# Seven products of a column-block pair summed in three PSUM banks that are read in between

## The chip, the core and the metric

The kernel runs on one core of a Trainium2 chip. The metric is the device time of one execution in microseconds (us): the median of three runs of the kernel before is 2645.06 us (2643.67 to 2646.84).

## The reference

The reference is a decoder trunk of two layers over one sequence of 1024 tokens with 1024 features, in float32. Each layer has a mixer and a gated MLP, both behind an RMSNorm that is shifted, scaled and gated by columns computed from a conditioning vector (adaLN).

```python
proj = h @ w_in                       # mixer: 4 retention heads, 4 HGRN2 heads, 128 wide
rq, rk, rv, rg, hq, hf, hi, hg = jnp.split(proj, idx, axis=-1)
...
merged @ w_out
...
a = h @ w_gate                        # MLP, 2816 wide
acc = causal_conv3(a) + conv_b
(jax.nn.silu(acc) * (h @ w_val)) @ w_down
```

Nearly all the arithmetic lies in `h @ w_in`, `h @ w_gate` and `h @ w_val`: every 128 columns of such a weight give 128 features for 1024 tokens.

## The kernel before

Activations are held feature-major: 128 features on the partitions, 1024 tokens along a row, in tiles Z of 128 x 1024 (12 of them, handed out and given back in a first-in, first-out list). Every operand of a large matmul is split exactly into two parts (hi and lo), so that a block of 128 x 128 weights against 512 tokens takes three matmuls: hi by hi, hi by lo, lo by hi (L451 to L453).

Most column blocks are computed in pairs. `pair` (L456) takes two blocks of 128 columns, a "gate" block g and a "value" block v, and gets their products with all 1024 tokens by seven products of halves in place of eight (the scheme of Strassen and Winograd). The halves of the activation (`b11`, `b12`, `b21`, `b22`) and their sums (`tops[1]` to `tops[3]`) are prepared once per norm by `sum_operands` and `last_operand`. The halves of the weights and their sums are made for each pair: GpSimd adds (L463 to L469), and `piece` (L324 on) splits each of the seven with one ScalarE copy (L329) and one VectorE subtraction (L330) into a rotation of six buffers. The raw weights of the two blocks come by two DMAs on SP's queue into two buffers, which are free again when the last split that reads them is done.

A product (`product`, L447) is 12 matmuls of 128x128 by 128x512 that are summed in one PSUM bank. I call the products P1 to P7 after the weight piece that they use. The banks come from a rotation of four (`pr_ps`); four more (`at_ps`) serve the mixer's small matmuls. In an ordinary pair the order is P1, P6, P2, P7, P4, P5, P3. P1 is copied to v0 by ScalarE (L491); each later result is added on VectorE to a half of g or v (L485), P5 twice (L485, L510). The first pair of each MLP has `plain_first` set: its order is P1, P2, P3, P6, P7, P4, P5, since the sums of the operands come late there; P3 is copied too (L497), and GpSimd does one add (L501). There are 68 pairs, 34 in each layer: 14 in the mixer, 20 in the MLP.

After each result `step` (L384) lets other work go on: a tick of the adaLN sums (VectorE, L165 and L167, for the columns that come later; they run through the first layer's mixer and MLP only) and the next part of the attention chains. `hgrn_chain` (L661) works on the pair f (as g) and q (as v); it has seven score levels, each with TensorE matmuls (L712, L722), a VectorE selection (L714) or ScalarE copy (L724), and two VectorE products (L730, L731). `ret_chain` (L621) turns the pair q, k by rotary (L613 to L618) and then multiplies them (L638). `value_chain` transposes the values. In the MLP `conv_act` (L950 on) takes g through a convolution (ScalarE L954, VectorE L955 and L957, ScalarE L959), multiplies it by v (L965) and stores the result in DRAM; the down projection (`slot_mm`, L526 to L528) loads it again and splits it (L531, L532).

The order of the instructions on each engine is set by the framework's scheduler when the program is made: it simulates the program and puts on each engine what is ready first, the earlier in the program and the work marked `hp()` (weights, copies and adds of the pairs) ahead of the rest. On the chip every engine then works through its own queue in that fixed order, and a wait holds up what stands behind it. The framework adds the waits: an instruction that writes a tile or a bank waits for those that still read it.

Of the kernel before, what the change touches and what calls it, by code (L numbers as in the profile page):

```python
# [29 lines left out]
HALF = 512  # L30
# [10 lines left out]
def kernel(  # L41
# [33 lines left out]
    def pr_ps(name):  # L75
        return psum.tile([P, HALF], F32, tag="pr", name=name)
# [25 lines left out]

# [1 line left out]
    vec_c0 = [("c", c_in.rearrange("b (r p) -> (b r) p", p=P), 8)]  # L104
# [37 lines left out]

# [1 line left out]
    mod = const.tile([P, DEPTH * 48], F32, name="mod")  # L144
# [69 lines left out]

# [1 line left out]

# [107 lines left out]

# [1 line left out]
    def piece(src, n, nm):  # L326
        hi = stg.tile([P, HALF], F32R, tag="whi", bufs=NW, name=f"whi{nm}")
        lo = stg.tile([P, HALF], F32R, tag="wlo", bufs=NW, name=f"wlo{nm}")
        A.activation(hi[:, 0:n], src, AF.Copy)  # L329
        V.tensor_tensor(out=lo[:, 0:n], in0=src, in1=hi[:, 0:n], op=ALU.subtract)  # L330
        return [(hi[:, i:i + P], lo[:, i:i + P]) for i in range(0, n, P)]
# [45 lines left out]
    def need(n):  # L377
        for _ in range(100):
            if len(zfree) >= n:
                return  # L380
            step()
        raise RuntimeError(f"{len(zfree)} of {n} tiles free")
# [27 lines left out]

# [1 line left out]
    def split(dst, k, src):  # L412
# [33 lines left out]

    def product(w, b, nm):  # L447
        ps = pr_ps(nm)
        for k in range(4):
            (wh, wl), rh, rl = w[k], b[0][:, k, :], b[1][:, k, :]  # L450
            T.matmul(ps, wh, rh, start=k == 0, stop=False)  # L451
            T.matmul(ps, wh, rl, start=False, stop=False)  # L452
            T.matmul(ps, wl, rh, start=False, stop=k == 3)  # L453
        return ps

    def pair(src_g, src_v, nm, plain_first=False):  # L456
        rg = load_raw(src_g, KT, nm + "g")
        rv = load_raw(src_v, KT, nm + "v")
        a11, a12, a21, a22 = rg[:, 0:HALF], rg[:, HALF:S], rv[:, 0:HALF], rv[:, HALF:S]
        s1 = stg.tile([P, HALF], F32, tag="s1", bufs=2, name=f"s1{nm}")  # L460
        with hp():
            p1 = piece(a11, HALF, nm + "1")
            G.tensor_add(s1, a21, a22)  # L463
            G.tensor_sub(a21, a11, a21)
            G.tensor_sub(a11, s1, a11)
            if not plain_first:
                p6 = piece(a11, HALF, nm + "6")
            p2 = piece(a12, HALF, nm + "2")
            G.tensor_sub(a12, a12, a11)  # L469
            if plain_first:  # L470
                p3 = piece(a12, HALF, nm + "3")
                p6 = piece(a11, HALF, nm + "6")
            p7 = piece(a21, HALF, nm + "7")
            p4 = piece(a22, HALF, nm + "4")
            p5 = piece(s1, HALF, nm + "5")
            if not plain_first:
                p3 = piece(a12, HALF, nm + "3")
        need(2)
        g, v = Z(), Z()
        g0, g1, v0, v1 = g.t[:, 0:HALF], g.t[:, HALF:S], v.t[:, 0:HALF], v.t[:, HALF:S]  # L480

        def add(o, x, w, b, i):
            ps = product(w, b, f"{nm}_{i}")
            with hp():
                V.tensor_add(o, x, ps)  # L485
            step()
            return ps

        m1 = product(p1, b11, nm + "_1")
        with hp():  # L490
            A.activation(v0, m1, AF.Copy)  # L491
        step()
        if plain_first:
            add(g0, v0, p2, b21, 2)
            m3 = product(p3, b22, nm + "_3")
            with hp():
                A.activation(g1, m3, AF.Copy)  # L497
            step()
            add(v0, v0, p6, tops[2], 6)
            with hp():  # L500
                G.tensor_add(g1, g1, v0)  # L501
            add(v1, v0, p7, tops[3], 7)
        else:
            add(g1, v0, p6, tops[2], 6)
            add(g0, v0, p2, b21, 2)
            add(v1, g1, p7, tops[3], 7)
        add(v0, v1, p4, b12, 4)
        m5 = add(v1, v1, p5, tops[1], 5)
        with hp():
            V.tensor_add(g1, g1, m5)  # L510
        if not plain_first:
            add(g1, g1, p3, b22, 3)
        return g, v
# [19 lines left out]

# [1 line left out]
    def transpose8(src, nm, evac):  # L535
# [222 lines left out]

# [1 line left out]
    xs = [Z() for _ in range(KT)]  # L760
# [85 lines left out]
    for l in range(DEPTH):  # L846
# [1 line left out]
        early = []  # L848
# [95 lines left out]

# [1 line left out]
        ada_all()  # L946
# [49 lines left out]

# [1 line left out]
        places = (sum([slots(b) for b in (b11, tops[2], b21, tops[3])], []), sum([slots(b) for b in (b12, b22, b11, b21)], []),  # L998
# [142 lines left out]
```

## Time and profile before

| | |
|---|---|
| median of 3 runs | 2645.06 us |
| the profiled execution: span from its first to its last instruction | 2637.6 us |
| TensorE matmul busy | 2519.4 us, 96% |
| VectorE busy | 1839.7 us, 70% |
| ScalarE busy | 986.1 us, 37% |
| GpSimd busy | 592.0 us, 22% |
| mean granted TensorE clock | 0.980 |

The profiled execution's own time is known by its span; what lies around the span (launch and end) is not in it. Engines are named PE (TensorE matmul), PEld (its weight load), DVE (VectorE), ACT (ScalarE), POOL (GpSimd) and SP. L451 is line 451 of the kernel. Matmuls are pipelined: one of 128x128 by 128x512 is shown as 0.39 us long, but they begin 0.23 us apart. In a row, the part behind the arrow in brackets names the instruction that ended the engine's idle time.

### The profile page before, as it was taken

Reading aid. Unit: us, or ns where it says so; the run is one execution under the profiler, and the core shown is the slowest. Engines: PE = TensorE matmul, PEld = TensorE weight load, DVE = VectorE, ACT = ScalarE, POOL = GpSimd, SP = SyncE. Lnnn points to the kernel's source line nnn. Section 1 sums busy time; section 2 is a strip of 40 time slices with the busy share of each in tenths; the row PEclk is TensorE's granted clock in tenths of the full one; section 3 lists DMA queues with packets and bytes.
Section 4 is the critical chain, followed back from the end, with each engine's and each line's share of the span. In section 5 each row is a group of like instructions: output and inputs, shape, how many; then the busy total and the mean of one; then the engine's idle time right before and its main releaser. Section 6 shows DMA issues by size and latency. Waiting matters only on the chain.

```text
span 2637.6 us, 32740 instructions
## 1 busy us (share of the span) xinstructions
PE 2519.4 (96%) x12189; PEld 2072.7 (79%) x12189; DVE 1839.7 (70%) x2781; ACT 986.1 (37%) x1685; POOL 592.0 (22%) x480
## 2 busy tenths in 40 slices
PE   5889999999999999899999899999999999999998
PEld 4777877877788888788877788888877888887887
DVE  6988788765987788834377777777387677674435
ACT  4533433333533333412264334444154333342224
POOL 1512223210423323200023222222033332320000
PEclk8999999999999999999999999999999999999999
DMA  8222322552234344732231112224212222254213
GB/s 293 69 86 86 104 77 82 174 187 80 71 121 132 126 140 151 245 125 94 86 108 56 50 39 64 73 73 160 92 56 76 84 76 88 80 198 138 96 53 107
DMA packets 293920, 283.56 MB, mean 108 GB/s; under 512 B 10793, under 2 KB 240769, under 8 KB 293761
## 3 DMA queue, kind: packets, MB, share of 16 engines
q1 hardware_dynamic: 275904, 219.42, 26.7%
q0 software_dynamic: 17408, 61.88, 6.5%
q8 instruction: 96, 1.57, 0.2%
q14 instruction: 63, 0.52, 0.1%
q10 hardware_dynamic: 449, 0.17, 0.0%
HBM read 229.00 MB, written 52.43 MB: 107 GB/s over the span
## 4 chain that ended last, share of the span: by engine, by line
PE 71%; DVE 12%; issue 10%; POOL 4%; DMA 2%; ACT 2%; POOLq 0%; SPq 0%; DVEq 0%; ACTq 0%
PE f L451 6%; PE f L453 6%; PE f L452 6%; PE dn L528 4%; PE dn L526 4%; PE dn L527 4%; PE lh L712 2%; PE wo L526 2%; PE wo L528 2%; PE wo L527 2%; PE g L451 2%; PE g L452 2%; PE g L453 2%; PE dn_last L526 2%; PE dn_last L528 2%
## 5 line engine op out<-in xcount | busy, mean ns | idle before, releaser
L451 PE MATMUL f<-hhi,whif 128*128 128x512 f32 x640 | 253.8, 397 | 1.9 <-DVE z L485 1.8
L453 PE MATMUL f<-hhi,wlof 128*128 128x512 f32 x640 | 251.4, 393 | 0.0
L452 PE MATMUL f<-hlo,whif 128*128 128x512 f32 x640 | 250.1, 391 | 0.0
L485 DVE TENSOR_TENSOR z<-z,f 128x512 f32<-128x512 f32 x238 | 161.5, 682 | 63.1 <-PE f L453 54.0
L451 PE MATMUL f<-thi,whif 128*128 128x512 f32 x480 | 190.2, 396 | 6.0 <-ACT z L491 4.0
L452 PE MATMUL f<-tlo,whif 128*128 128x512 f32 x480 | 190.0, 396 | 0.0
L453 PE MATMUL f<-thi,wlof 128*128 128x512 f32 x480 | 189.7, 395 | 0.0
L528 PE MATMUL dn<-hhi,wlodn 128*128 128x512 f32 x384 | 151.8, 395 | 9.8 <-DVE wlodn L330 9.8
L526 PE MATMUL dn<-hhi,whidn 128*128 128x512 f32 x384 | 151.6, 395 | 0.0
L527 PE MATMUL dn<-hlo,whidn 128*128 128x512 f32 x384 | 150.1, 391 | 0.0
L167 DVE SCALAR_TENSOR_TENSOR ac<-aw,cact,ac 128x512 f32<-128x512 f32 x140 | 130.7, 934 | 22.8 <-DMA aw<-in_ada_w_dram 22.0
L912 DVE SCALAR_TENSOR_TENSOR z<-dn,mod,z 128x512 f32<-128x512 f32 x64 | 48.0, 750 | 136.3 <-PE dn L528 136.1
L453 PEld LDWEIGHTS f<-hhi,wlof 128*128 128x128 f32 x640 | 120.7, 189 | 28.4
L451 PEld LDWEIGHTS f<-hhi,whif 128*128 128x128 f32 x640 | 120.5, 188 | 28.3 <-DVE z L485 2.3
L452 PEld LDWEIGHTS f<-hlo,whif 128*128 128x128 f32 x640 | 120.6, 188 | 26.9
L451 PEld LDWEIGHTS f<-thi,whif 128*128 128x128 f32 x480 | 90.6, 189 | 29.7 <-ACT z L491 4.9
L915 POOL DMA_DIRECT2D xd<-z x48 | 26.0, 541 | 390.4 <-DVE z L912 362.5
L329 ACT ACTIVATE whidn<-rawdn 128x512 fp32r<-128x512 f32 x64 | 39.5, 627 | 186.1 <-PE dn L527 173.3
L453 PEld LDWEIGHTS f<-thi,wlof 128*128 128x128 f32 x480 | 90.6, 189 | 20.9
L452 PEld LDWEIGHTS f<-tlo,whif 128*128 128x128 f32 x480 | 90.2, 188 | 20.6
L712 PEld LDWEIGHTS lh<-z,z 128*128 128x128 f32 x640 | 80.1, 199 | 24.1 <-issue 19.6
L712 PE MATMUL lh<-z,z 128*128 128x64 f32 x640 | 80.1, 280 | 17.1 <-DVE z L731 16.3
(664 smaller groups left out, 6868.7 us busy)
## 6 DMA issues: line engine op xcount, KB each, us to landing
aw<-in_ada_w_dram SPq DMA_DIRECT2D x160, 256.0 KB, 2.7
acts<-z POOLq DMA_DIRECT2D x44, 512.0 KB, 3.2
z<-acts SPq DMA_DIRECT2D x44, 512.0 KB, 4.3
z<-xd POOLq DMA_DIRECT2D x32, 512.0 KB, 5.7
rawdn<-in_w_down_dram SPq DMA_DIRECT2D x32, 512.0 KB, 3.8
xd<-z POOLq DMA_DIRECT2D x52, 256.0 KB, 2.7
rawdn_last<-in_w_down_dram SPq DMA_DIRECT2D x32, 384.0 KB, 3.4
af<-in_ada_w_dram SPq DMA_DIRECT2D x16, 512.0 KB, 9.9
```

Of the source, the lines that this page charges most:

```text
L167: V.scalar_tensor_tensor(out=a, in0=raw, scalar=cact[:, k:k + 1], in1=a, op0=ALU.mult, op1=ALU.add)
L329: A.activation(hi[:, 0:n], src, AF.Copy)
L451: T.matmul(ps, wh, rh, start=k == 0, stop=False)
L452: T.matmul(ps, wh, rl, start=False, stop=False)
L453: T.matmul(ps, wl, rh, start=False, stop=k == 3)
L485: V.tensor_add(o, x, ps)
L526: T.matmul(ps, a, rh, start=i == 0, stop=False)
L527: T.matmul(ps, a, rl, start=False, stop=False)
L528: T.matmul(ps, b, rh, start=False, stop=i == last)
L712: T.matmul(ps[:, c * 64:(c + 1) * 64].rearrange("p (b t) -> p b t", t=s), k.t[:, cs], qp.t[:, cs].rearrange("p (b t) -> p b t", t=s)[:, 1: ...
L912: V.scalar_tensor_tensor(out=x, in0=ps, scalar=mod[:, l * 48 + gate + d:][:, 0:1], in1=x, op0=ALU.mult, op1=ALU.add)
L915: nc.gpsimd.dma_start(out=dst[d, :, sl], in_=x)
```

## The change

`product` gives way to `add_product`, which writes into a bank that it is given and may add to what the bank holds. A pair takes three banks, x, w and y (with `plain_first` a fourth, u). x takes P1, is copied to g0, then takes P6 on top and is copied to g1, takes P7 on top and is added to v1, takes P4 on top and is copied to v0. w takes P2, which is added to g0. y takes P5 and is copied to v1, takes P3 on top and is added to g1. So an ordinary pair has four ScalarE copies and three VectorE adds. The order of the products becomes P1, P2, P6, P5, P7, P3, P4; with `plain_first` it is P1, P2, P3, P6, P5, P7, P4, with P3 in u and four adds. The weight splits stand in the new order. `step` is still called after each result. Comments that the diff removes elsewhere are left out here.

```diff
@@ -444,14 +444,12 @@
             split(b12, k, xs[4 + k].t[:, 0:HALF])
             xs[4 + k].free()
 
-    def product(w, b, nm):
-        ps = pr_ps(nm)
+    def add_product(ps, w, b, first=True, last=True):
         for k in range(4):
             (wh, wl), rh, rl = w[k], b[0][:, k, :], b[1][:, k, :]
-            T.matmul(ps, wh, rh, start=k == 0, stop=False)
-            T.matmul(ps, wh, rl, start=False, stop=False)
-            T.matmul(ps, wl, rh, start=False, stop=k == 3)
-        return ps
+            T.matmul(ps, wh, rh, start=first and k == 0, stop=False, skip_group_check=True)
+            T.matmul(ps, wh, rl, start=False, stop=False, skip_group_check=True)
+            T.matmul(ps, wl, rh, start=False, stop=k == 3, skip_group_check=True)
 
     def pair(src_g, src_v, nm, plain_first=False):
         rg = load_raw(src_g, KT, nm + "g")
@@ -463,53 +461,53 @@
             G.tensor_add(s1, a21, a22)
             G.tensor_sub(a21, a11, a21)
             G.tensor_sub(a11, s1, a11)
-            if not plain_first:
-                p6 = piece(a11, HALF, nm + "6")
             p2 = piece(a12, HALF, nm + "2")
             G.tensor_sub(a12, a12, a11)
             if plain_first:
                 p3 = piece(a12, HALF, nm + "3")
-                p6 = piece(a11, HALF, nm + "6")
+            p6 = piece(a11, HALF, nm + "6")
+            p5 = piece(s1, HALF, nm + "5")
             p7 = piece(a21, HALF, nm + "7")
-            p4 = piece(a22, HALF, nm + "4")
-            p5 = piece(s1, HALF, nm + "5")
             if not plain_first:
                 p3 = piece(a12, HALF, nm + "3")
+            p4 = piece(a22, HALF, nm + "4")
         need(2)
         g, v = Z(), Z()
         g0, g1, v0, v1 = g.t[:, 0:HALF], g.t[:, HALF:S], v.t[:, 0:HALF], v.t[:, HALF:S]
 
-        def add(o, x, w, b, i):
-            ps = product(w, b, f"{nm}_{i}")
+        def out(o, ps):
             with hp():
-                V.tensor_add(o, x, ps)
+                A.activation(o, ps, AF.Copy)
             step()
-            return ps
-
-        m1 = product(p1, b11, nm + "_1")
-        with hp():
-            A.activation(v0, m1, AF.Copy)
-        step()
+
+        def add(o, ps):
+            with hp():
+                V.tensor_add(o, o, ps)
+            step()
+
+        x, w, y = pr_ps(nm + "_x"), pr_ps(nm + "_w"), pr_ps(nm + "_y")
+        add_product(x, p1, b11)
+        out(g0, x)
+        add_product(w, p2, b21)
+        add(g0, w)
         if plain_first:
-            add(g0, v0, p2, b21, 2)
-            m3 = product(p3, b22, nm + "_3")
-            with hp():
-                A.activation(g1, m3, AF.Copy)
-            step()
-            add(v0, v0, p6, tops[2], 6)
-            with hp():
-                G.tensor_add(g1, g1, v0)
-            add(v1, v0, p7, tops[3], 7)
-        else:
-            add(g1, v0, p6, tops[2], 6)
-            add(g0, v0, p2, b21, 2)
-            add(v1, g1, p7, tops[3], 7)
-        add(v0, v1, p4, b12, 4)
-        m5 = add(v1, v1, p5, tops[1], 5)
-        with hp():
-            V.tensor_add(g1, g1, m5)
+            u = pr_ps(nm + "_u")
+            add_product(u, p3, b22)
+        add_product(x, p6, tops[2], False)
+        out(g1, x)
+        if plain_first:
+            add(g1, u)
+        add_product(y, p5, tops[1])
+        out(v1, y)
+        if plain_first:
+            add(g1, y)
+        add_product(x, p7, tops[3], False)
+        add(v1, x)
         if not plain_first:
-            add(g1, g1, p3, b22, 3)
+            add_product(y, p3, b22, False)
+            add(g1, y)
+        add_product(x, p4, b12, False)
+        out(v0, x)
         return g, v
 
     def slots(b):
```

## Rows read from the trace of the kernel before

**Rows 1.** The page: span, and busy times (us, share, instructions).

```profile
span 2637.6 us, 32740 instructions
PE 2519.4 (96%) x12189; PEld 2072.7 (79%) x12189; DVE 1839.7 (70%) x2781; ACT 986.1 (37%) x1685; POOL 592.0 (22%) x480
```

**Rows 2.** Windows, mixers then MLPs: us, PE, PEld, DVE, ACT, POOL, clock, DMA.

```profile
112.00:480.00 368.00, 339.48 (x2061) 288.19 (x2062) 304.52 (x523) 133.23 (x286) 92.77 (x59) 0.97 0.31 95
1410.00:1770.00 360.00, 337.73 (x2042) 286.83 (x2041) 266.71 (x461) 134.96 (x289) 90.22 (x59) 0.98 0.18 56
760.00:1060.00 300.00, 299.79 (x1336) 245.18 (x1335) 247.43 (x330) 100.11 (x150) 94.32 (x75) 1.00 0.44 140
2010.00:2350.00 340.00, 340.00 (x1473) 276.82 (x1472) 236.35 (x300) 120.24 (x175) 107.16 (x90) 1.00 0.28 91
```

**Rows 3.** TensorE's waits, whole span: waited for, us in total, times, longest.

```profile
PE lh L712 <- DVE z L731: 16.3, 8, 5.9
...
PE dn L528 <- DVE wlodn L330: 9.8, 2, 7.6
PE v L451 <- ACT z L491: 8.1, 2, 4.1
```

**Rows 4.** Busy times within one MLP pair: second layer, first layer (columns as above).

```profile
2176.50:2196.00 19.50, 19.50 (x86) 15.89 (x85) 13.48 (x17) 6.99 (x11) 6.15 (x5) 1.00 0.25 81
938.30:957.70 19.40, 19.40 (x90) 15.98 (x89) 16.22 (x21) 7.23 (x12) 6.16 (x5) 1.00 0.35 109
```

**Rows 5.** Groups, VectorE: adds of MLP pairs (busy us, mean ns).

```profile
L485 DVE TENSOR_TENSOR z<-z,f 128x512 f32<-128x512 f32 x238 | 161.5, 682 | 63.1 <-PE f L453 54.0 <-issue 7.5
```

**Rows 6.** Timeline: product after P1 begins, copy of P1; MLP 2, MLP 1.

```profile
2179.23 0.40 PE L451 MATMUL f<-thi,whif 128*128 128x512 f32 x1
...
2179.80 0.58 ACT L491 ACTIVATE z<-f 128x512 f32<-128x512 f32 x1
...
941.03 0.40 PE L451 MATMUL f<-thi,whif 128*128 128x512 f32 x1
...
944.84 0.57 ACT L491 ACTIVATE z<-f 128x512 f32<-128x512 f32 x1
```

**Rows 7.** Chain of waits, 1085 to 1112: start us, us, what.

```profile
1092.40 1.23 DVE z L965
...
1100.03 6.43 DMA z<-acts
```

**Rows 8.** Busy times and clock around two of TensorE's waits (columns as above).

```profile
1098.90:1113.30 14.40, 6.75 (x24) 5.09 (x23) 9.72 (x12) 3.24 (x3) 2.10 (x4) 0.76 0.79 295
...
207.00:219.00 12.00, 7.88 (x34) 6.58 (x33) 10.21 (x13) 2.32 (x4) 4.46 (x4) 0.72 0.11 44
```

**Rows 9.** Timeline of VectorE, value pair of head 1, second layer.

```profile
1503.21 1.29 DVE L676 COPY_PREDICATED z<-mkh,z 128x1024 f32<-128x1024 uint8 x1
```

**Rows 10.** Timeline of TensorE, first pair of the first layer.

```profile
109.97 1.11 PE L540 MATMUL tpr_0v<-ident,z 128*128 128x128 f32 x4 [5.32 <-ACT z L606]
```

**Rows 11.** Timeline of TensorE and ScalarE, first MLP pair of the first layer.

```profile
707.62 0.58 ACT L491 ACTIVATE z<-f 128x512 f32<-128x512 f32 x1
...
708.25 0.50 PE L451 MATMUL f<-thi,whif 128*128 128x512 f32 x1 [1.98 <-ACT z L491]
...
716.02 0.63 ACT L329 ACTIVATE whif<-rawf_3g 128x512 fp32r<-128x512 f32 x1 [7.30 <-POOL rawf_3g L465]
716.56 0.58 ACT L497 ACTIVATE z<-f 128x512 f32<-128x512 f32 x1
...
720.38 0.39 PE L451 MATMUL f<-hhi,whif 128*128 128x512 f32 x1
```

**Rows 12.** Timeline, f, q pair, second layer: P6, copy of P1, rotary.

```profile
1446.34 0.48 PE L451 MATMUL h<-thi,whih 128*128 128x512 f32 x1
...
1458.84 0.60 ACT L491 ACTIVATE z<-h 128x512 f32<-128x512 f32 x1 [3.21 <-DVE z L615]
...
1459.94 1.21 DVE L618 TENSOR_TENSOR z<-z,z 128x1024 f32<-128x1024 f32 x1
```

## The prediction

> **What bounds the kernel now.** I read the whole-run busy times first. TensorE is busy for 2519 of 2637.6 us, VectorE for 1840, ScalarE for 986 [rows 1]. That is a share over stages, so the table by stage came next [rows 2]. In the gated MLP of either layer TensorE is never idle (299.8 of 300 us, 340 of 340 us): nothing there can become faster than its matmuls, and the change keeps all 84 of a pair. In the two mixers TensorE is idle for 28.5 of 368 us and 22.3 of 360 us, while VectorE is busy for 83% and 74%. So the change can win in the mixers and at the borders between stages, and inside the MLP it can only lose. The list of what TensorE waited for names places [rows 3]: the score levels of the HGRN heads (L712 behind L731), the start of the down projection (L528 behind the weight split of L330) and the bank rotation of the pairs (L451 behind L491).
>
> **What a pair costs now.** A pair of the MLP takes TensorE 19.5 us, a product of 12 matmuls a seventh of it, 2.79 us [rows 4]. A VectorE add out of PSUM takes 0.68 us [rows 5], a ScalarE copy 0.58 us [rows 6]. An ordinary pair (66 of the 68) loses four adds and gains three copies: VectorE -2.73 us, ScalarE +1.73 us. The two pairs with plain_first go from six adds to four and from two copies to four, and lose one GpSimd add (L501). In all VectorE sheds 66 x 2.73 + 2 x 1.36 = 183 us and ScalarE takes on 66 x 1.73 + 2 x 1.16 = 117 us. Neither is on the path by itself. What counts is where VectorE's relief reaches TensorE, and what the new waits cost.
>
> **The new wait.** Today each product has a bank of its own out of four, so a result may be read up to three products late. After the change P6, P7 and P4 go into the bank of P1, and P3 into that of P5; each must wait until the copy or add before it has read the bank. Behind such a wait stands all of TensorE's queue, the mixer's small matmuls too. In an ordinary pair one other product, 2.79 us, lies between. In the MLP of the second layer the copy of P1 begins 0.57 us after the next product has begun and lasts 0.58 us [rows 6]: it is over 1.15 us into a product of 2.79 us, so I cost these waits at nothing. In the first layer it is over at 945.41, 4.4 us after P1 (941.03) [rows 6], 1.6 us too late. There VectorE is busy for 16.2 us of a pair, against 13.5 us in the second layer [rows 4]; the surplus is the adaLN column sums. With 2.7 us less it has 13.5 us, what the second layer has today with a lag of 0.57 us. So I take 2 us for the 19 ordinary pairs together, with 0 and 19 x 1.6 = 30 us as bounds.
> The Trainium skill (Perfetto Trace Analysis, Optimizing Tensor Performance, Matmuls) says that independent matmul groups should rotate through different PSUM banks, so that the reading of one overlaps the matmuls of the next. That speaks against writing the same bank again: were nothing overlapped, each of the four reuses would expose 1.15 us, some 310 us over 68 pairs, where the sum has nothing. The trace shows that the product in between covers a prompt reading [rows 4, 6], so the rule would bite only where the reading is late: the slower rival below.
>
> **Gains.** (a) Start of the down projection. TensorE waits 7.6 us in the first layer and the rest of 9.8 us in the second [rows 3]. In the first layer the chain of waits runs from L965, which writes a gate product at 1092.40, over its store to an operand load that needs the freed buffer and lands at 1106.46 [rows 7]. The gate column is now finished one product sooner (P3 before P4), 2.8 us, and VectorE is 2.7 us per pair less behind, which together is most of the wait. Next late are VectorE's operand splits, so I take 8 of 9.8 us. The granted clock was 0.76 over 14.4 us there [rows 8], a fall to 1.2 GHz after the idling that cost 3.5 us; 2 us of that returns. Gain 10 us, bounds 0 and 13.
> (b) The value pairs of head 1. TensorE waits 8.1 us in two places [rows 3], because the copy of P1 goes into a tile that L676 frees late (1503.21 + 1.29 in the second layer) [rows 9]. Now P1 goes into g, whose tile is free, and v is first written after the fourth product. The wait stays, but comes one product later: about 1.2 us is left of each 4. Gain 5.6 us, and with part of the clock's fall (0.72 over 12 us in the first layer [rows 8], 3.4 us) 8 us; bounds 0 and 12.
> (c) VectorE's relief in the mixers. The first layer's mixer has 304.5 - 266.7 = 37.8 us more VectorE work than the second's, and 6.2 us more idle TensorE [rows 2]: 0.16 us per us. Some twelve pairs lie in each window; 2 x 12 x 2.73 = 66 us less is worth 10 us. Bounds 0 and all the idle time, 50.8 us.
> (d) In the very first pair TensorE idles 5.3 us at 110 before P6 can begin [rows 10]; P2, which needs none of the sums, now stands ahead of P6 and fills part. Gain 2 us, bounds 0 and 2.8.
>
> **Losses.** (e) The first pair of each MLP (plain_first). The copy of P1 is over at 707.62 + 0.58 = 708.20; P6, which today begins in a bank of its own before that, must wait for it [rows 11]. Worse, the copy of P3 (L497) stood on ScalarE behind a weight split that waited for GpSimd until 716.02. If the new copy of P6 stands there, P7 begins at 717.2 (today at 708.25, behind the copy of P1), P4 must then wait for the add of P7 with nothing in between, 1.1 us, and ends at 724.1, where today the next pair begins at 720.38. That is 3.7 us, and with some matmuls at 1.2 GHz after the idling 5 us, twice: 10 us, bounds 2 and 20.
> (f) The f, q pair of head 1. Its copy of P1 waited until 1458.84 for the rotary (L615) without harm, since P6 had begun at 1446.34 in a bank of its own [rows 12]. Now g takes the tile that the later L618 frees (1459.94 + 1.21 = 1461.15), and P6 must wait for the copy: 1461.9 at worst, with two products done where the fourth is nearly over today, 4.9 us. q is finished one product sooner, which pulls the rotary forward, but it runs behind other work. I take 4 us in each layer, 8 us, bounds 0 and 16.
> (g) In the first pair of each mixer VectorE is late, and P4 now waits for the add of P7. 3 us, bounds 0 and two products, 5.6.
> (h) The late copies above: 2 us, bounds 0 and 30.
> Without cost: the weight splits change their order with the products. P3's split moves from seventh to sixth, so the gate block's buffer is free one product sooner; P4's is last and frees the value block's where the gate block's is freed today. SP issues the two loads in the same order and GpSimd waits for the second as before. The cover is that weights are split most of a pair ahead; if it were gone, P6's split would cost its lateness.
>
> **Sum.** Gains 10 + 8 + 10 + 2 = 30, losses 10 + 8 + 3 + 2 = 23: 7 us less. The profiled execution spans 2637.6 us, 7.5 us below the median of 2645.06; what lies around the span is untouched, so the span should be 2631 and the median **2638 us**.
>
> **Rivals.** Less than 0.2%, 5.3 us, can't be told from no change here. *Cancelled*: the relief (c) does not reach TensorE, which is busy for 96% and takes in its idle time whatever is ready. Without (c) the sum is 3 us more than today: 2648. For it: the MLPs have nothing to give [rows 2]. Chance 0.28.
> *Late copies, slower*: the copies stand on ScalarE behind a weight split or a convolution step that waits for VectorE or GpSimd, as L497 does behind L329 [rows 11] and L491 in the first layer's MLP [rows 6]. It decides from 2.2 us of lag on (2.79 - 0.58). If the first layer's lag stays, 28 us come on top of (h): 2666. Against it: the second layer's lag of 0.57 us under the VectorE load that the first will have [rows 4, 6]. Chance 0.24. The rule of the Trainium skill named above (Perfetto Trace Analysis) would have this one happen.
> *Large relief*: the mixers wait on VectorE in chains (L731 [rows 3]), half of their 50.8 us of idle time goes, 15 us more than (c), and (f) costs half: 2619. Chance 0.09.
> The forecast itself: 0.39.
>
> **How the numbers follow.** Faster is forecast and large relief, 0.48; same is cancelled, 0.28; slower 0.24. The range reaches down to large relief and a little more, 2617, and up to most of late copies, 2662: about 0.12 is left out above and 0.05 below. The faster cases alone lie between 2617 and 2640.
>
> **What would show it.** VectorE should have 206 adds for the pairs where L485 and L510 have 474, and ScalarE 272 copies where L491 and L497 have 70; VectorE busy for about 1657 us, ScalarE for 1103. Right: L528's wait under 2 us, VectorE near 13.5 us per pair in the first layer's MLP, no wait of P6 or P7 there. Wrong: matmuls of P6, P7, P3 or P4 waiting for copies pair after pair in either MLP, or the mixers' idle TensorE not below 50 us; a plain_first pair that takes no longer than today would strike (e).

## The result, and the profile after

The kernel after takes **2801.01 us** (median of 4 runs, 2796.78 to 2805.99) where the kernel before takes 2644.36 (4 runs): a ratio of **1.0594**, 95% interval 1.0581 to 1.0607. That is slower by 157 us; forecast were 7 us less, and the range ended at 2662.

The page of the kernel after, span and busy times; they answer to [rows 1]:

```profile
span 2804.2 us, 32500 instructions
...
PE 2585.7 (92%) x12189; PEld 2117.0 (75%) x12189; DVE 1686.5 (60%) x2513; ACT 1086.3 (39%) x1883; POOL 565.4 (20%) x478
```

VectorE shed 153 us and ScalarE took on 100, where 183 and 117 were worked out. TensorE has as many matmuls as before, is busy for 66 us more, and still idles for 100 us more. TensorE's waits in the kernel after (waited for, us in total, times, longest; L450 to L452 are now the matmuls of a product, L480 the copies, L485 the adds):

```profile
PE f_y L450 <- ACT z L480: 73.1, 34, 8.3
PE f_x L450 <- ACT z L480: 19.9, 6, 5.2
...
PE f_x L450 <- DVE z L485: 11.3, 4, 3.4
...
PE v_y L450 <- ACT z L480: 7.4, 2, 3.8
```

f_y is the bank y of an MLP pair. P3 waits there for ScalarE's copy of P5, in 34 of the 38 ordinary pairs of the MLPs: what the prediction had named as the sign of its being wrong. The waits of L528 at the start of the down projection [rows 3] are gone. The stages tell where the time went, in us from the first matmul of a stage to the first of the next (worked out from the traces; the last row goes to the start of the last matmul of the down projection; the stretches between a mixer and the first pair of its MLP, 142 to 143 us in each of these kernels, are left out; the last two columns are kernels of the experiments):

| stage | before | after | held_to_g1 | all_repaired |
|---|---|---|---|---|
| mixer 1 | 451.8 | 470.0 | 460.1 | 452.8 |
| MLP 1, 20 pairs | 404.4 | 475.9 | 424.3 | 420.2 |
| down projection 1, start of layer 2 | 308.0 | 299.9 | 306.8 | 309.0 |
| mixer 2 | 429.4 | 441.7 | 435.0 | 430.0 |
| MLP 2, 20 pairs | 392.5 | 468.8 | 401.0 | 391.6 |
| down projection 2 | 251.9 | 247.9 | 247.9 | 248.0 |

The two MLPs lose 71.5 and 76.3 us, the mixers 30.5 together. Busy times over 18 of the 19 ordinary pairs of the second MLP, from the start of its second pair to that of its last; the same view is used for every kernel below (columns as in [rows 2]). The kernel before:

```profile
2001.80:2351.10 349.30, 349.30 (x1513) 284.44 (x1512) 244.31 (x310) 124.33 (x180) 108.53 (x91) 1.00 0.28 91
```

and the kernel after:

```profile
2104.50:2516.20 411.70, 372.49 (x1513) 296.58 (x1512) 191.38 (x234) 152.00 (x235) 102.17 (x90) 0.95 0.27 77
```

A pair went from 19.4 to 22.9 us. Of the 62.4 us, 39.2 are idle TensorE, and 23.2 are matmuls that last longer at a lower clock (0.95). Now one pair of them, which begins at 2329.4, and the next, from 2352.5: the timeline of the kernel after, engine by engine, cut to the instructions that hand on to each other (start, duration, engine, line; in brackets the idle time before it and what ended it):

```profile
2344.14 0.63 ACT L329 ACTIVATE whif<-rawf_14g 128x512 fp32r<-128x512 f32 x1 [5.40 <-POOL rawf_14g L463]
2344.68 0.58 ACT L480 ACTIVATE z<-f_y 128x512 f32<-128x512 f32 x1
...
2345.31 0.49 PE L450 MATMUL f_y<-hhi,whif 128*128 128x512 f32 x1 [1.90 <-ACT z L480]
...
2349.95 0.69 DVE L485 TENSOR_TENSOR z<-z,f_y 128x512 f32<-128x512 f32 x1 [2.75 <-PE f_y L452]
...
2350.68 1.24 ACT L952 ACTIVATE z<-z,cols,cols 128x1024 f32<-128x1024 f32 x1 [0.27 <-DVE z L485]
...
2351.95 1.29 DVE L953 SCALAR_TENSOR_TENSOR z<-z,cols,z 128x1023 f32<-128x1023 f32 x1 [0.71 <-ACT z L952]
...
2353.81 1.28 DVE L955 SCALAR_TENSOR_TENSOR z<-z,cols,z 128x1022 f32<-128x1022 f32 x1
...
2355.18 1.06 ACT L957 ACTIVATE z<-z 128x1024 f32<-128x1024 f32 x1 [1.53 <-DVE z L955]
2356.14 0.58 ACT L480 ACTIVATE z<-f_x 128x512 f32<-128x512 f32 x1
2356.62 0.63 ACT L329 ACTIVATE whif<-rawf_14v 128x512 fp32r<-128x512 f32 x1
...
2357.41 0.68 DVE L330 TENSOR_TENSOR wlof<-rawf_14v,whif 128x512 fp32r<-128x512 f32 x1
...
2358.13 0.37 SPq L340 DMA_DIRECT2D rawf_15v<-in_w_val_dram  x1
...
2363.35 1.28 POOL L461 TENSOR_TENSOR s1f<-rawf_15v 128x512 f32<-128x512 f32 x1 [4.98 <-DMA rawf_15v<-in_w_val_dram]
2364.71 1.30 POOL L462 TENSOR_TENSOR rawf_15v<-rawf_15g,rawf_15v 128x512 f32<-128x512 f32 x1
2366.09 1.27 POOL L463 TENSOR_TENSOR rawf_15g<-s1f,rawf_15g 128x512 f32<-128x512 f32 x1
...
2367.38 0.63 ACT L329 ACTIVATE whif<-rawf_15g 128x512 fp32r<-128x512 f32 x1 [5.52 <-POOL rawf_15g L463]
```

Read it as a **loop**. ScalarE waits 5.4 us for GpSimd with the split of the *next* pair's P6 block (L329). Right behind it in the queue stands the copy of P5 (L480), which could have run at 2340.6, when P5's last matmul (begun at 2340.22, 0.39 us long) was over. So P3 begins 1.90 us late and ends late, and so do the last add of the gate block, the convolution (L952 to L957), P4's split behind it, the load of the next value block that needs the buffer which this split frees, GpSimd's three sums, and the split of the pair after. From 2344.14 to 2367.38 it is 23.2 us, the length of the pair (23.1). That TensorE could do a pair in 19.4 us doesn't matter.

### The profile page after: what moved, and what is told of

The parts are those of the page before. It is cut to its first block, busy times and chain, and to the rows that moved or that the text cites. A ratio compares the mean times of both kernels' runs of the same rounds, so it can differ in the third digit from the quotient of the medians.

```text
span 2804.2 us, 32500 instructions
## 1 busy us (share of the span) xinstructions
PE 2585.7 (92%) x12189; PEld 2117.0 (75%) x12189; DVE 1686.5 (60%) x2513; ACT 1086.3 (39%) x1883; POOL 565.4 (20%) x478
## 5 line engine op out<-in xcount | busy, mean ns | idle before, releaser
L450 PE MATMUL f_x<-thi,whif 128*128 128x512 f32 x320 | 129.9, 406 | 19.9 <-ACT z L480 19.9
L167 DVE SCALAR_TENSOR_TENSOR ac<-aw,cact,ac 128x512 f32<-128x512 f32 x140 | 119.1, 851 | 45.8 <-DMA aw<-in_ada_w_dram 44.9
L450 PE MATMUL f_y<-hhi,whif 128*128 128x512 f32 x152 | 75.7, 498 | 73.1 <-ACT z L480 73.1
L450 PE MATMUL f_x<-hhi,whif 128*128 128x512 f32 x320 | 129.6, 406 | 11.3 <-DVE z L485 11.3
L451 PE MATMUL f_x<-tlo,whif 128*128 128x512 f32 x320 | 128.9, 403 | 0.0
L452 PE MATMUL f_x<-thi,wlof 128*128 128x512 f32 x320 | 128.8, 403 | 0.0
L451 PE MATMUL f_x<-hlo,whif 128*128 128x512 f32 x320 | 128.2, 400 | 0.0
L452 PE MATMUL f_x<-hhi,wlof 128*128 128x512 f32 x320 | 127.9, 400 | 0.0
L329 ACT ACTIVATE whidn<-rawdn 128x512 fp32r<-128x512 f32 x64 | 40.2, 628 | 194.1 <-PE dn L525 178.6
L450 PEld LDWEIGHTS f_y<-hhi,whif 128*128 128x128 f32 x152 | 34.8, 229 | 94.5 <-ACT z L480 87.4
L913 POOL DMA_DIRECT2D xd<-z x48 | 26.0, 541 | 394.9 <-DVE z L910 366.9
L450 PEld LDWEIGHTS f_x<-thi,whif 128*128 128x128 f32 x320 | 62.1, 194 | 36.7 <-ACT z L480 22.5
L526 PEld LDWEIGHTS dn<-hhi,wlodn 128*128 128x128 f32 x384 | 72.1, 188 | 16.7
L525 PEld LDWEIGHTS dn<-hlo,whidn 128*128 128x128 f32 x384 | 72.1, 188 | 16.1
L524 PEld LDWEIGHTS dn<-hhi,whidn 128*128 128x128 f32 x384 | 72.2, 188 | 15.5
```

The source lines that it names most:

```text
L167: V.scalar_tensor_tensor(out=a, in0=raw, scalar=cact[:, k:k + 1], in1=a, op0=ALU.mult, op1=ALU.add)
L450: T.matmul(ps, wh, rh, start=first and k == 0, stop=False, skip_group_check=True)
L451: T.matmul(ps, wh, rl, start=False, stop=False, skip_group_check=True)
L452: T.matmul(ps, wl, rh, start=False, stop=k == 3, skip_group_check=True)
L524: T.matmul(ps, a, rh, start=i == 0, stop=False)
L525: T.matmul(ps, a, rl, start=False, stop=False)
```

## The experiments

In each diff, only what differs from the kernel named stands. The two parts of a split are called hi (ScalarE) and lo (VectorE). "Issued after" is an order that the scheduler is told to keep in an engine's queue. Theory A was at first: the copy of P5 is late since it stands behind a split that waits. Rival B: a bank that is written again after one product is too tight in any case.

**split_held**: the kernel after, with the order of two queues changed. `held` has the copy of P5 and the add of P7 of the pair before.

```diff
-            p6 = piece(a11, HALF, nm + "6")
+            p6 = piece(a11, HALF, nm + "6", True)  # hi issued after held[0], lo after held[1]
-        out(v1, y)
+        held.append(out(v1, y))
-        add(v1, x)
+        held.append(add(v1, x))
```

> Only the order of two queues changes: the split of the next pair's P6 block stands on ScalarE behind the copy out(v1,y), and on VectorE behind the add(v1,x). Theory A (the copy of P5 and the add of P7 are late because the next pair's P6 split stands ahead of them in the queue and waits for GpSimd): the waits f_y <- ACT z of 73.1 us go to under 10, ordinary MLP pairs go from 23 to 19.4-20 us, 38 pairs x 3.6 us = 136 us, so about 2665 us (2640 to 2690). Rival B (a bank written again with one product between is too tight even when it is read promptly): P3 goes on waiting 1 us and more in each pair, and the time stays at 2800 +- 15. Rival C (the half clock after each wait has another cause than the wait): the waits go, the half clock stays, some 80 us less, about 2720.

2697.73 us, 1.0209 of the kernel before (1.0183 to 1.0235): 103 of 157 us are back. What is left of the waits for copies, and the 18 pairs:

```profile
PE f_x L458 <- ACT z L489: 23.9, 19, 5.2
...
PE f_y L458 <- ACT z L489: 4.5, 1, 4.5
```

```profile
2042.90:2402.00 359.10, 352.56 (x1513) 283.07 (x1512) 187.13 (x233) 148.57 (x233) 103.22 (x90) 1.00 0.31 88
```

The same banks are reused as before, and the clock is back at 1.00: rivals B and C fall. But 359.1 is not 349.3, and the time is 8 us over the range.

**p3_in_w** and **copy5_on_dve**: P3 in another bank, or P5 read by another engine.

```diff
-            add_product(y, p3, b22, False)
             add(g1, y)
+            add_product(w, p3, b22)
+            add(g1, w)
```

```diff
-        out(v1, y)
+        V.tensor_copy(out=v1, in_=y); step()
```

> P3 goes into the bank of P2, which has been free for three products, with an add of its own, so that it can't wait for the copy of P5. Theory A: ScalarE and VectorE stay blocked by the split, so P4, in the bank of P7, waits for the add of P7 instead, 2 to 3 us a pair: f_y's wait of 73 us goes and a wait on VectorE of 70 to 100 us comes; 2800 us +- 20. Rival B (the bank of P5 with one product between is what is too tight): the waits go and nothing comes: 2670 to 2700.

> The copy of P5 is made by VectorE, ahead of the lo part of the next P6 split in its queue, and so before VectorE's own wait. Theory A: P3 no longer waits, but P4 does, for the add of P7, which still stands behind the split on VectorE: f_y's 73 us go to under 15, f_x's wait for VectorE comes to 70 to 100 us, time 2800 +- 20. Rival B: P3 waits as before; 2800. If ScalarE's queue alone were at fault: about 2670.

2726.54 and 2723.25 us (one run each). The new wait came as expected, on VectorE, since the lo part of the same split stands ahead of the add of P7 there:

```profile
PE f_x L450 <- DVE z L485: 62.0, 35, 5.6
```

is p3_in_w's; copy5_on_dve has 42.0 us in 31 places. It is smaller than the wait that went (73.1), and the two kernels gave back 74 and 78 us where I expected none; 34 of p3_in_w's 74 us lie in the mixers, which the expectation left out. The expected 2 to 3 us a pair are what P4 waits in four pairs of the kernel after, late in each MLP, where the copy of P5 stands ahead of the split, as here:

```profile
2487.94 0.50 PE L450 MATMUL f_x<-hhi,whif 128*128 128x512 f32 x1 [2.72 <-DVE z L485]
```

p3_in_w also brings the mixers to 449.0 and 428.7 us, about the kernel before's length, and the three later kernels with P3 in w in their mixers have 452.5 to 457.8 and 423.8 to 430.0: the mixers' loss comes from P3 in the bank of P5.

**value_first**: the value block is loaded and freed ahead of the gate block.

```diff
-        rg = load_raw(src_g, KT, nm + "g")
         rv = load_raw(src_v, KT, nm + "v")
+        rg = load_raw(src_g, KT, nm + "g")
...
+            p4 = piece(a22, HALF, nm + "4")
             if not plain_first:
                 p3 = piece(a12, HALF, nm + "3")
-            p4 = piece(a22, HALF, nm + "4")
```

> The value block is loaded ahead of the gate block and P4's split is made ahead of P3's, so that GpSimd's chain begins with the gate block's landing and its first sum is already made: the P6 block is ready 1.3 us earlier, nothing else is moved. Theory A: P3's wait shrinks by as much, from 2.2 to 0.9 us a pair, 36 x 1.3 = 47 us and part of the half clock: about 2740 us (2700 to 2765). Rival B: the wait doesn't hang on the load: 2800 +- 15.

2703.14 us (one run), 98 us less where 61 were expected: the split of P4 now stands ahead of the convolution's last step, so more than 1.3 us fell out. No bank and no read was touched.

**own_banks**: the new order of products and splits, but a bank for each product.

```diff
+        copy(v0, own(p1, b11, 1))
+        sums(g0, v0, own(p2, b21, 2))
+        sums(g1, v0, own(p6, tops[2], 6))
+        m5 = own(p5, tops[1], 5)
+        sums(v0, g1, own(p7, tops[3], 7))
+        V.tensor_add(v1, v0, m5); V.tensor_add(g1, g1, m5)
+        sums(g1, g1, own(p3, b22, 3))
+        sums(v0, v0, own(p4, b12, 4))
```

> The new order of products and of splits stays, but each product has a bank of its own again, with 1 copy and 7 adds (the first pair of the MLP in the old form). Theory A (late reads hurt only because a bank is written again after one product; the split that blocks ScalarE is harmless when four banks rotate): the MLP pairs are back at 19.4 to 20.3 us, the mixers at 451 and 429, and the start of the down projection keeps its gain (308 to 300 and 252 to 248 us): 2632 us (2625 to 2645). Rival D (the new order of the splits, with the value block freed later, is itself the loss): P6 or P5 wait for their weights, 2690 and more.

2771.0 us, 1.0471 (1.0440 to 1.0502). This is where theory A, which blamed the late read *of a reused bank*, fell. ScalarE's P6 splits of two pairs, and VectorE and TensorE behind the second:

```profile
2295.04 0.63 ACT L329 ACTIVATE whif<-rawf_13g 128x512 fp32r<-128x512 f32 x1 [6.57 <-POOL rawf_13g L463]
...
2316.75 0.63 ACT L329 ACTIVATE whif<-rawf_14g 128x512 fp32r<-128x512 f32 x1 [6.59 <-POOL rawf_14g L463]
...
2317.41 1.21 DVE L330 TENSOR_TENSOR wlof<-rawf_14g,whif 128x512 fp32r<-128x512 f32 x1 [5.86 <-ACT whif L329]
2318.54 0.67 DVE L489 TENSOR_TENSOR z<-z,f 128x512 f32<-128x512 f32 x1
...
2319.36 0.47 PE L450 MATMUL f<-hhi,whif 128*128 128x512 f32 x1 [2.06 <-DVE z L489]
```

The adds stand behind the lo part of the split, the gate block ends late, and the loop closes over the convolution and the load as above, without TensorE in it: 21.7 us from split to split, 21.8 a pair. TensorE waits at the next pair's first product. So I formed theory E: the loop sets the pair's length, and the banks only decide where TensorE pays. Rival D: the new order costs by itself.

**own_held** and **own_value_first**: own_banks with the lo part of the split issued after the add `g1 += m5`, or with value_first's edit.

```diff
-            V.tensor_add(g1, g1, m5)
+            held.append(V.tensor_add(g1, g1, m5))  # the lo part of the next P6 split is issued after it
```

> As own_banks, but the lo part of the next pair's P6 split stands on VectorE behind the adds of P7 and P5. Theory E (in own_banks and after, the pair's length is that of a loop that closes outside of TensorE: P6 split, the reads that stand behind it, the end of the gate block, the convolution on ScalarE, P4's split behind it, the load of the next value block, GpSimd's three sums, the next P6 split; 21.7 us in own_banks, 2295.04 to 2316.75): the loop is cut where the reads stand behind the split, TensorE bounds again, MLP pairs of 19.4 to 20.3 us, no wait f <- DVE z; about 2635 us (2625 to 2650) if the mixers are also at 451 and 430, 2665 if they stay at 471 and 444. Rival D (the order of products or splits costs in itself, whatever stands behind what): 2700 and more.

> As own_banks, with the value block loaded first and P4's split ahead of P3's, and so ahead of the convolution's last step on ScalarE. Theory E: the same loop, shorter by the Silu step, the copy and the place in the load queue (3 to 4 us of 21.7), falls below TensorE's 19.4: MLP pairs 19.4 to 20, 2640 to 2680 us. Rival D: 2750 and more.

own_held: 2693.93 us, 1.0194 (1.0177 to 1.0211). Its 18 pairs:

```profile
2056.50:2405.10 348.60, 348.60 (x1513) 284.79 (x1512) 240.21 (x309) 124.86 (x180) 108.37 (x90) 1.00 0.29 91
```

The loop is cut where theory E says, and TensorE never idles in these pairs. The total is 29 us over the upper figure, as the mixers stayed at 477.8 and 440.5 and the first MLP is 416.6: for these stages own_held doesn't strike rival D. own_value_first: 2735.03 us (one run), 383.7 us for the 18 pairs: shorter than own_banks by 9.6, but still a loop of 21.3 us; the 3 to 4 us that I thought to take out were 0.5, for P4's split came ahead of the Silu and the gate block's load then came last.

**before_p4_last**: the kernel before with P4's split last.

```diff
-            p4 = piece(a22, HALF, nm + "4")
             p5 = piece(s1, HALF, nm + "5")
             p3 = piece(a12, HALF, nm + "3")
+            p4 = piece(a22, HALF, nm + "4")
```

> The kernel before with P4's weight split last of the seven, as in the change, and nothing else. Theory E: with the products in the old order the gate block isn't behind the split's wait by more than its slack (VectorE waits 0.87 us for TensorE ahead of the last add of a pair) and P4's split stands ahead of the convolution's Silu; the loop stays under 19.4: 2644 us +- 8. Rival D (a value block freed last is the loss by itself): 2 us a pair and more, 2700.

2666.24 us, 1.0091 (1.0076 to 1.0106): 22 us, where theory E said none and rival D 56. The second MLP does keep its 349.3 us; the 22 lie in the first layer's MLP (413.3 against 404.4), the first mixer (457.7 against 451.8) and in small amounts elsewhere. So the order of splits costs something of its own, though not in the loop.

**gp_in_after, gp_in_held, gp_in_before**: GpSimd's first sum made twice in each MLP pair, 1.36 us more, in three kernels.

```diff
-            G.tensor_add(s1, a21, a22)
+            for _ in range(2 if nm[0] == "f" else 1):
+                G.tensor_add(s1, a21, a22)
```

> The kernel after, with GpSimd's first sum of each MLP pair made twice (the second time with the same result): 1.3 us more of GpSimd's work ahead of the next P6 split, 40 times; GpSimd is busy 20% of the time. Theory E (the loop through GpSimd sets the pair's length): each ordinary MLP pair is 1.3 us longer, 36 to 38 of them, so 47 to 50 us: about 2850 us (2835 to 2865). Rival F (GpSimd is off the path and the waits come from the banks alone): no change, 2801 +- 10.

> The same sum made twice in the kernel with the P6 split held behind the reads. Theory E: the loop is cut, so the 40 x 1.3 us are hidden: 2698 us, up to 2713 where the slack was under 1.3 us. Rival F: no change either; if the split held is still late for P6, as the wait of 0.59 us ahead of P6 in the second MLP lets think, up to 40 us more.

> The same sum made twice in the kernel before. Theory E: the loop is there too, but some 2 us shorter than TensorE's 19.4 us (the adds wait 0.87 and 2.1 us for TensorE), so that 1.3 us fit in: 2644 us, up to 2660 in the first MLP, where 10 of 20 pairs last 20.3. If 1.3 us a pair show, 2690, the kernel before had no slack and any later value block would have cost as much.

2877.25, 2748.82 and 2673.2 us: 76 us over after, 51 over split_held, 30 over before (1.0114, 1.0098 to 1.0129). All three lie above what theory E gave, by 12, 36 and 13 us. The 18 pairs, in gp_in_after,

```profile
2131.70:2583.30 451.60, 387.87 (x1513) 308.14 (x1512) 191.23 (x234) 151.90 (x234) 124.82 (x108) 0.91 0.25 70
```

in gp_in_held,

```profile
2064.10:2452.00 387.90, 361.80 (x1514) 289.02 (x1513) 189.06 (x234) 149.58 (x235) 126.70 (x108) 0.97 0.29 82
```

and in gp_in_before:

```profile
2030.40:2379.70 349.30, 349.30 (x1513) 284.42 (x1512) 232.65 (x304) 120.43 (x180) 127.78 (x108) 1.00 0.28 90
```

In the kernel after, an engine that is busy 20% of the time is on the path: idle TensorE grows by 24.5 us (63.7 against 39.2), which is 18 x 1.36 to the tenth, and 15.4 us come as slower matmuls. In the kernel before the same work is hidden there to the tenth; its 30 us lie mostly in the first layer's MLP (429.8 against 404.4), where nearly all of 20 x 1.36 us shows: the kernel before had almost no slack there (I put that down to the adaLN sums; it was not tested). The miss is gp_in_held: 28.8 us in 18 pairs, so the loop was not cut. VectorE's queue in split_held shows why: the add of P3 into the gate block still stood behind the split, though TensorE had gone on from P3 to P4 at 2297.91.

```profile
2298.15 1.24 DVE L338 TENSOR_TENSOR wlof<-rawf_16g,whif 128x512 fp32r<-128x512 f32 x1 [2.04 <-ACT whif L336]
2299.31 0.68 DVE L338 TENSOR_TENSOR wlof<-s1f,whif 128x512 fp32r<-128x512 f32 x1
2299.91 0.67 DVE L495 TENSOR_TENSOR z<-z,f_y 128x512 f32<-128x512 f32 x1
```

**held_to_g1** and **held_to_g1_gp**: the lo part behind that add as well, alone and with GpSimd's sum twice.

```diff
-        held.append(add(v1, x))
+        add(v1, x)
...
-            add(g1, y)
+            held.append(add(g1, y))
```

> As split_held, but on VectorE the lo part of the P6 split stands behind the last add of the gate block (P3's) instead of the add of P7, so that nothing between TensorE's last gate product and the convolution stands behind GpSimd. Theory E: the rest of the loop that gp_in_held showed (51 us for 52 us of work) is cut: the wait of P6 for the copy of P1 (23.9 us, 19 times, in split_held) goes down to 10 or less, MLP pairs of the second layer are 19.4 instead of 19.9: 2685 us (2675 to 2695). If the loop was cut already in split_held: 2698 as there.

> The same with GpSimd's first sum made twice. Theory E: now the 1.3 us are outside of any loop and hidden, as in the second layer of the kernel before: up to 10 us over held_to_g1, in pairs of 19.4 to 20 us in the second layer. If 40 to 50 us come back: GpSimd's lateness reaches TensorE in yet another way, and the account of the loop is not complete.

2674.4 us, 1.0113 (1.0096 to 1.0130), and 2678.39 (1.0134, 1.0113 to 1.0154). The 18 pairs of the first and of the second:

```profile
2045.00:2393.40 348.40, 348.40 (x1513) 284.55 (x1512) 185.48 (x234) 155.66 (x234) 108.11 (x90) 1.00 0.29 91
```

```profile
2046.50:2395.10 348.60, 348.60 (x1514) 284.42 (x1512) 185.77 (x234) 153.91 (x234) 131.49 (x108) 1.00 0.29 91
```

Now GpSimd's extra work is free and TensorE is never idle, with three banks, two of them written again after one product. Only queue order differs from the kernel after. That settles the loop in the second layer. In the first layer's MLP the 18 pairs take 366.9 and 368.6 us (409.7 in the kernel after, 357.8 before), so most of it is back there too. The waits of f_x for copies still come to 22.6 us, where 10 or less were expected, but in 6 places, four of them in the first MLP pairs.

**repaired** and **all_repaired**: split_held, or held_to_g1, with the first MLP pair in the old form and P3 in w in the mixers.

```diff
+        if plain_first:
...
+            return g, v
+        mlp = nm[0] == "f"
+        if not mlp:
+            add(g1, y)
+            y = w
-        add_product(y, p3, b22, False)
+        add_product(y, p3, b22, not mlp)
```

> The kernel after with three repairs: MLP pairs with the P6 split held behind the reads, mixers with P3 in the bank of P2, the first MLP pair in the old form with a bank for each product. If the loss is the sum of these places: mixers 449 and 429 (17 and 10 us below split_held), first MLP pairs 26 and 24 instead of 34.5 and 27.6, so 2697.7 - 27 - 12 = about 2659 us (2645 to 2675). If something else of the change costs time: it stays above 2680.

> The change with all the places repaired that the runs have shown: held_to_g1 in the MLP's ordinary pairs, the first MLP pair in the old form with a bank for each product (34.3 and 33.2 us there, 25.8 and 23.8 in the kernel before), P3 in the bank of P2 in the mixers (460 and 435 us there, 449 and 429 in p3_in_w). If the loss is the sum of these places: 2674.4 - 18 - 17 = 2640 us (2632 to 2652), so no gain over the kernel before is left in the change, though VectorE makes 3 or 4 adds a pair where it made 7. If VectorE's relief is worth what the prediction thought (10 us and more): 2630 or below. If a further loss is hidden: 2655 and more.

2674.61 us (one run), at the upper end of its range, and 2654.69, 1.0053 (1.0039 to 1.0067), 3 us over it. By the table of stages the mixers and the second layer are as before or 4 us better. What is left is the first layer's MLP, 15.8 us. The trace of all_repaired shows 14.6 us of them as waits for bank x: 8.1 us in four places for the add of P7, 6.5 us in three for a copy. The adds stand in VectorE's queue behind an adaLN sum (L167) that waits for a load, for example here:

```profile
781.59 0.75 DVE L167 SCALAR_TENSOR_TENSOR ac<-aw,cact,ac 128x512 f32<-128x512 f32 x1 [1.10 <-DMA aw<-in_ada_w_dram]
782.26 0.68 DVE L529 TENSOR_TENSOR z<-z,f_x 128x512 f32<-128x512 f32 x1
...
782.99 0.80 PE L458 MATMUL f_x<-hhi,whif 128*128 128x512 f32 x1 [2.79 <-DVE z L529]
```

So here too a read of a bank that is written again stands behind an instruction that waits. No run moved these adds. No gain of the change outweighs the loss.

**before_last** and **mixer_w_last_pair**: the kernel before with P5 and P3 ahead of P4 in each MLP's last pair; and that with p3_in_w's sums in the mixers.

```diff
+        if last:
+            m5 = add(g1, g1, p5, tops[1], 5)
+            add(g1, g1, p3, b22, 3)
+            add(v0, v1, p4, b12, 4)
+            V.tensor_add(v1, v1, m5)
+            return g, v
```

> The kernel before, with one pair per layer changed: in the MLP's last pair P5 and P3 come ahead of P4, each in a bank of its own, so that the gate block is complete one product earlier and the convolution starts 2.8 us earlier. If the down projection's wait at its start (9.8 us, rows 3) is set by the gate block's end, 2 x 2.8 = 5.6 us are gained: about 2639. If the start is set by the store and load behind it alone, the same. If the value pair's late end takes it back: 2644 or more.

> What the runs so far leave as a version ahead of both: the MLP of the kernel before with P5 and P3 ahead of P4 in its last pair (2638.4 us), and in the mixers the change's sums in PSUM with P3 in the bank of P2 (449.0 and 428.7 us against 451.8 and 429.4). Sum: 2638.4 - 2.8 - 0.7 = 2635 us (2628 to 2645). If the mixers' 3 us were noise: 2638.

2638.4 us, **0.9979 (0.9968 to 0.9990)**, and 2638.41, 0.9986 (0.9976 to 0.9995). Both are ahead of the kernel before, by 0.2% and 0.1%, with intervals that end below 1; the mixers' part adds nothing that can be told. In before_last TensorE's waits at the start of the two down projections come to 4.6 us where they were 9.8 [rows 3], which fits the 5 us; the two profiled executions differ by only 0.7 us.

## Why the prediction was wrong

The step that failed is **the new wait**, with term (h) and the line "Without cost". It put a price on four reads by the lag of one: in [rows 6] the only copy that then stood on ScalarE, that of P1, begins 0.57 us late in the second MLP, and from that "I cost these waits at nothing". The copy of P5 stands at another place in the queue, behind a split that already waited 5.75 us for GpSimd in the kernel before, where nothing that TensorE needed soon stood behind it:

```profile
2189.24 1.15 ACT L329 ACTIVATE whif<-rawf_13g 128x512 fp32r<-128x512 f32 x2 [5.75 <-POOL rawf_13g L465]
...
2193.10 0.63 ACT L329 ACTIVATE whif<-rawf_13v 128x512 fp32r<-128x512 f32 x1 [2.16 <-PE f L452]
...
2196.81 1.25 ACT L954 ACTIVATE z<-z,cols,cols 128x1024 f32<-128x1024 f32 x1 [0.26 <-DVE z L485]
```

The second row is P4's split, ahead of the convolution (L954). And "GpSimd waits for the second as before" took the split order for neutral: P4's split now frees the value block, and stands behind the convolution's last step. Together they close the loop. Measured: 51.9 and 62.4 us in the 18 ordinary pairs of the two MLPs, 11.9 and 5.7 in the last pairs (32.7 and 25.1 us against 20.8 and 19.4), where (h) had 2 us within 0 and 30. Without the loop, in all_repaired, the late reads that (h) is about cost 14.6 us, inside its bounds.

The rival *Late copies* had the right mechanism, even the queue ("behind a weight split ... that waits for VectorE or GpSimd"), at a fifth of its price: 28 us, in the first layer only. It was bounded by the prompt reading of the second layer; a lateness that feeds back through the load isn't bounded by any row of the kernel before. The Trainium skill's rule of rotating banks (Perfetto Trace Analysis, Optimizing Tensor Performance, Matmuls) pointed the right way, but names the smaller part: own_banks follows it and stays 4.7% slower, held_to_g1 breaks it and its second MLP runs at 19.4 us a pair. The Trainium skill (Perfetto Trace Analysis, Per-engine timelines, Tensor Engine Instruction) also says that ScalarE, VectorE and GpSimd are strictly first in, first out; the copy at 2344.68, ready since 2340.6, agrees.

The other terms:
- (a) Start of the down projection, a gain of 10: L528's waits went, and the two stages are 8.1 and 4.0 us shorter, but the last pairs ahead of them grew. In held_to_g1 and all_repaired the second layer's last pair and down projection are 4 us shorter (267.3 against 271.3), the first layer's not. So 4, not 10.
- (b) Value pairs of head 1, a gain of 8: v's wait is 7.4 us where it was 8.1 [rows 3], and the two pairs are 3.0 and 0.1 us shorter. So 3 at most.
- (c) Mixers, a gain of 10: they lost 30.5 us in all. In p3_in_w, where P3 doesn't wait, with 3 of the 4 adds still gone from VectorE, they are 2.8 and 0.7 us shorter than before, but a mixer of the same instructions varies by more than that from one kernel's profile to the next: 447.9 to 451.8 and 429.4 to 430.6 with the old sums (before, before_last, gp_in_before), 449.0 to 457.8 and 423.8 to 430.0 with p3_in_w's (four kernels). So no gain from VectorE's relief can be told in the mixers; *Cancelled* had this right.
- (d) The very first pair, a gain of 2: TensorE's wait of 5.3 us [rows 10] is 3.5 us, so 1.8 came back there; the pair as a whole is longer, see (g).
- (e) First MLP pairs, a loss of 10 within 2 to 20: 33.5 and 32.0 us against 25.8 and 23.8, so 15.9. The two waits that it was built on are there: 5.2 us each for the copy of P1, 4.1 and 3.6 for that of P6.
- (f) and (g), 11 us together: the f, q pairs of head 1 became shorter (49.3 and 50.0 against 56.7 and 55.5, 12.9 us), the mixers' first pairs longer (44.9 and 34.9 against 36.1 and 24.9, 18.8 us). Sum 5.9: a cancellation, not a hit; what lengthened the first pairs was not tested.
- VectorE's pair in the MLPs is as worked out: 248 us over 18 pairs of the first layer, 13.8 us (13.5 forecast). That it was right shows how little it was worth.

## What to carry to other kernels

Price a read that is moved by what stands ahead of it in its queue at that place, and not by the lag of another read on the same engine. Then look for loops that close outside the bounding engine (a read, what it releases, a load, the next split): their length against the bounding engine's period is the slack, and some work doubled on an idle engine in the loop shows whether there is any. A few instructions put in another order on one queue may be worth more than the work that a change takes away.

## What the runs showed that I had not expected

The waits cost more than their length. In the pair shown above, clock and busy times of the kernel after in the stretch with the wait, and in P3's stretch behind it:

```profile
2340.60:2345.30 4.70, 2.81 (x13) 1.92 (x11) 0.50 (x1) 1.16 (x3) 4.46 (x4) 1.00 0.00 0
2345.30:2349.20 3.90, 3.89 (x11) 3.09 (x12) 1.90 (x3) 0.48 (x1) 0.15 (x1) 0.60 0.02 4
```

After 1.90 us without a matmul the granted clock averages 0.60 over P3, so most of it ran at 1.2 GHz, and P3 lasted 4.4 us in place of 2.8. In 10 of the 16 pairs of the second MLP in which P3 waits for the copy it lasts 4.1 to 4.5 us, after 1.8 to 2.8 us of idling; in the other 6 it lasts 2.9, after 1.3 to 2.0 us. Since P3 is in the loop, that too lengthens the next wait. And the same 1.36 us on GpSimd cost 76, 51, 30 or 4 us in a whole kernel, depending on what stands behind it in the queues.
